# A hybrid decoder step on one core: the samples' value window put together in DRAM

## The chip, the core and the metric

The kernel runs on one core of a Trainium2 chip. Five engines work from queues of their own, each strictly in order: TensorE (PE, with its weight loads PEld), VectorE (DVE), ScalarE (ACT), GpSimd (POOL) and SyncE (SP), which here issues every DMA. The metric is the device time of one execution in microseconds (us), lower is better.

## What is computed

One inference step of two layers. Layer 0 runs sliding-window attention (8 query heads, 2 key/value heads of width 64, window 128, a learned sink per head) beside a gated delta rule; layer 1 is gated linear attention. A prompt of 2048 tokens (with 16 meta tokens in front) and 8 samples of one new token each go through both. What the change touches is the samples' attention and the cache it returns:

```python
def _swa_sample(q, k_new, v_new, k_buf, v_buf, sink):        # k_buf, v_buf: (8, 128, 2, 64)
    k = jnp.concatenate([k_buf.astype(k_new.dtype), k_new], axis=1)
    v = jnp.concatenate([v_buf.astype(v_new.dtype), v_new], axis=1)
    ...
    mask = (diff >= 0) & (diff < WINDOW)                     # the new row and the last 127 of the cache
    o = _sink_attend(q, k, v, mask, sink)
    return o.reshape(Bn, T, A_HEADS, A_HEAD_DIM), k[:, T:], v[:, T:]
```

So for each of the 8 samples a window of 128 value rows (128 floats each) is needed twice: as an operand of the attention, with a row on each partition, and as an output.

## The kernel before

The prompt is worked in four groups of 512 columns; group 0 also carries the 8 samples and 16 meta tokens, so its tiles have 536 columns, in two halves of 268. Per group: layer 0's projections (`ab_head`, `ab_rest`: key, convolution, query and gate blocks), its output projection (`ab_out`), then layer 1 (`c_main`, `c_out`). A projection (`proj`) is float32 in three passes: a weight tile is loaded raw (L270), split by ACT (L275, `wh`) and POOL (L278, `wl`, printed as L112 in the profile because a helper emits it), multiplied by PE into one of four PSUM buffers `pp`, and evacuated by DVE. In group 0 each split weight is also stored to DRAM (L245, `wd`) for the later groups. The weight pool has 8 buffers, so a raw load waits until PE is through with a tile from some blocks before.

Side work runs as generators between the blocks of a projection (`spawn`, `bulk`, with due times in `DEF_LAT`). The framework then lays out each engine's queue with a scheduler of its own, so an edit can shift instructions far from it. [...]

The samples' attention is `swa_extra`, spawned in group 0 while the fourth query and gate blocks are projected. For each half of the samples it loads the cached keys transposed (L495, `kc`, 128 partitions), then 127 cached value rows of 4 samples into partitions 0 to 126 (L498, `vc`), and then the 4 new value rows from partitions 4x to 4x+3 of `vs` into partition 127 (L499). Scores use `kc` (L527), the weighted values use `vc` (L548). Near its end it writes the outputs: cached rows 1 to 127 of each sample DRAM to DRAM (L562 for keys, L563 for values) and the new rows (L564, L570); the scheduler put L562 and L563 early, at 67.9 and 120.9 us. The new value rows `vs` come out of `ab_v` (L705), the projection of values that is evacuated at about 41 us.

Right behind L499 on SP stand the loads of the output projection: the residual X tiles (L991, 8 of 268 KB) and the raw weights of `w_abo` in two stages: 256 of 1024 columns of each of 8 blocks first, then 768 of each. In the second stage SP also stores each finished block (L1016, `x1d`).

Of the kernel before, what the change touches and what calls it, by code (L numbers as in the profile page):

```python
# [9 lines left out]
F32 = mybir.dt.float32  # L10
# [10 lines left out]
SMP = 8  # L21
# [47 lines left out]
def kernel(ctx: ExitStack, tc: tile.TileContext, ins, outs):  # L69
    nc = tc.nc  # L70
    V, A, G, T, SY = nc.vector, nc.scalar, nc.gpsimd, nc.tensor, nc.sync
# [3 lines left out]
    dr = ctx.enter_context(tc.tile_pool(name="dr", bufs=2, space=bass.MemoryType.DRAM))  # L75
# [6 lines left out]
    def nm(s):  # L82
        cnt[0] += 1
        return f"{s}_{cnt[0]}"
# [11 lines left out]
    def t512(shape=(128, 128), dt=F32):  # L96
        return wk.tile(list(shape), dt, tag="t512", bufs=4, name=nm("t5"))
# [4 lines left out]
    def cb(shape=(128, 512)):  # L102
        return pc.tile(list(shape), F32, tag="pc", name=nm("pc"))
# [4 lines left out]
    def MM(out, lhsT, rhs, start=True, stop=True):  # L108
        T.matmul(out, lhsT, rhs, start=start, stop=stop)  # L109

    def TT(out, a, b, op, eng=None):
        (eng or V).tensor_tensor(out, a, b, op=op)  # L112
# [13 lines left out]
    def bcm(ap, n):  # L126
        return ap.unsqueeze(1).to_broadcast([ap.shape[0], n] + list(ap.shape[1:]))
# [227 lines left out]
    def until(cond):  # L355
        while not cond():
            yield 0.5, 0.0
# [113 lines left out]
    def swa_extra(q, gx):  # L471
        vt = q.vt

        vm, vs = vt["m"], vt["s"]
        sc = cb()
        for h in range(8):
            MM(sc[0:16, 16 * h:16 * h + 16], QX[:, h, SMP:EX], KX[:, h // 4, SMP:EX])
        S3 = t512((128, 8, 16))[0:16]
        TT(S3, sc[0:16, 0:128].rearrange("p (h k) -> p h k", h=8), bcm(CC[0:16, C_MSK + 128:C_MSK + 144], 8), add)
        st = sm((128, 32))[0:16]  # L480
        V.tensor_reduce(st[:, 0:8], S3, axis=AX.X, op=amax)
        TT(st[:, 0:8], st[:, 0:8], RV[0:16, 0:8], amax)
        TT(S3, S3, bc(st[:, 0:8], 16), sub)
        A.activation(S3, S3, AF.Exp)
        TT(st[:, 8:16], RV[0:16, 0:8], st[:, 0:8], sub)
        A.activation(st[:, 8:16], st[:, 8:16], AF.Exp)
        V.tensor_reduce(st[:, 16:24], S3, axis=AX.X, op=add)
        TT(st[:, 16:24], st[:, 16:24], st[:, 8:16], add)
        V.reciprocal(st[:, 24:32], st[:, 16:24])
        TT(S3, S3, bc(st[:, 24:32], 16), mul)  # L490
        yield from take_in("T", 5)
        kc, vc = ([ft(shape=(128, 4, 128)) for _ in range(2)] for _ in range(2))
        for x in range(2):
            b4 = slice(4 * x, 4 * x + 4)
            SY.dma_start(kc[x][:, :, 0:127], ins["kcT"][:, b4])  # L495
            for kv in range(2):
                V.tensor_copy(kc[x][64 * kv:64 * kv + 64, :, 127], KX[:, kv, 4 * x:4 * x + 4])
            SY.dma_start(vc[x][0:127], ins["cv"][b4, 1:128, :].rearrange("b k d -> k b d"))  # L498
            SY.dma_start(vc[x][127:128, :, :], vs[4 * x:4 * x + 4, :])  # L499
        QZ = ft(shape=(128, 512))  # L500
        V.memset(QZ, 0.0)
        for kv in range(2):
            r = slice(64 * kv, 64 * kv + 64)
            dst = QZ[r, 0:504].rearrange("p (b x) -> p x b", x=72)[:, 4 * kv:4 * kv + 4, :]
            V.tensor_copy(dst, QX[:, 4 * kv:4 * kv + 4, 0:7])
            V.tensor_copy(QZ[r, 504 + 4 * kv:508 + 4 * kv], QX[:, 4 * kv:4 * kv + 4, 7])
        yield LAT["sx_1"], 0.3
        pt = cb()
        for h in range(8):
            T.transpose(pt[0:16, 16 * h:16 * h + 16], S3[:, h, :], ident[0:16, 0:16])  # L510
        PT = t512((128, 128))[0:16]
        A.copy(PT, pt[0:16, 0:128])
        yield LAT["sx_2"], 0.3
        po = cb()
        for kv in range(2):
            MM(po[64 * kv:64 * kv + 64, 0:64], vm[0:16, 64 * kv:64 * kv + 64], PT[:, 64 * kv:64 * kv + 64])
        yield from until(lambda: gx)
        for u in range(4):
            z = t512((128, 16))
            TT(z, po[:, 16 * u:16 * u + 16], GX[:, u, SMP:EX], mul)  # L520
            store_m0(q, u, z, SMP, META)

        yield 0.5, 0.1

        sc = cb()
        for b in range(8):
            MM(sc[0:64, 0:128], QZ[:, 64 * b:64 * b + 64], kc[b // 4][:, b % 4], start=(b == 0), stop=(b == 7))  # L527
        P = t512((128, 128))[0:64]
        st = sm((128, 8))[0:64]
        snk = PV[0:64, P_SNK:P_SNK + 1]  # L530
        V.tensor_copy(P, sc[0:64, 0:128])
        V.tensor_reduce(st[:, 0:1], P, axis=AX.X, op=amax)
        TT(st[:, 0:1], st[:, 0:1], snk, amax)
        TS(st[:, 1:2], st[:, 0:1], -1.0)
        A.activation(P, P, AF.Exp, bias=st[:, 1:2], accum_out=st[:, 2:3])
        A.activation(st[:, 3:4], snk, AF.Exp, bias=st[:, 1:2])
        TT(st[:, 2:3], st[:, 2:3], st[:, 3:4], add)
        V.reciprocal(st[:, 4:5], st[:, 2:3])
        TS(P, P, st[:, 4:5])
        yield LAT["sx_3"], 0.9  # L540
        pt = cb()
        T.transpose(pt[:, 0:64], P, ident[0:64, 0:64])
        PT = t512((128, 64))
        A.copy(PT, pt[:, 0:64])
        yield LAT["sx_4"], 0.1
        po = cb()
        for b in range(8):
            MM(po[:, 8 * b:8 * b + 8], vc[b // 4][:, b % 4], PT[:, 8 * b:8 * b + 8])  # L548
        pos = t512((128, 64))
        A.copy(pos, po[:, 0:64])  # L550
        pv = pos.rearrange("p (b h) -> p h b", b=8)
        for u in range(4):
            z = t512((128, 8))
            for kv in range(2):
                r = slice(64 * kv, 64 * kv + 64)
                TT(z[r], pv[r, 4 * kv + u, :], GX[r, u, 0:SMP], mul)
            store_m0(q, u, z, 0, SMP)

        give("T", 5)
        yield LAT["sx_5"], 0.9  # L560

        SY.dma_start(outs["ks"][:, 0:127, :], ins["ck"][:, 1:128, :])  # L562
        SY.dma_start(outs["vs"][:, 0:127, :], ins["cv"][:, 1:128, :])  # L563
        SY.dma_start(outs["vs"][:, 127, :], vs[0:8, :])  # L564
        kt_ = cb()
        for kv in range(2):
            T.transpose(kt_[0:8, 64 * kv:64 * kv + 64], KX[:, kv, 0:SMP], ident[0:64, 0:64])
        kn = t512((128, 128))[0:8]
        A.copy(kn, kt_[0:8, 0:128])
        SY.dma_start(outs["ks"][:, 127, :], kn)  # L570
# [110 lines left out]
    def ab_v(q):  # L681
        g, s0 = q.g, q.s0
        NS = 6 if g == 0 else 4
        BA = wk.tile([128, 6, 8], F32, tag="BA", bufs=2, name=nm("BA"))
        if g == 0:
            V.memset(BA, 0.0)
        q.vt = {}

        def ev_v(p2, slot):
            ps = t512((128, 136))  # L690
            A.copy(ps, p2[:, 136:272])
            TT(ps, ps, p2[:, 0:136], add)
            if g == 0:
                c = 4 if slot == "e" else slot
                TS(ps, ps, q.rst[:, c:c + 1])
            if slot == "e":
                e = wk.tile([128, 256], F32, tag="SM", bufs=4, name=nm("exv"))
                A.copy(e[0:EX, 0:136], ps[0:EX, 0:136])
                vm = wk.tile([128, 128], F32, tag="va", bufs=6, name=nm("vm"))
                V.memset(vm, 0.0)  # L700
                SY.dma_start(vm[0:META], e[SMP:EX, 0:128])
                SY.dma_start(BA[0:META, 0, :], e[SMP:EX, 128:136])
                V.tensor_copy(BA[0:SMP, 5, :], e[0:SMP, 128:136])
                vs = wk.tile([128, 128], F32, tag="va", bufs=6, name=nm("vs"))
                V.tensor_copy(vs[0:SMP], e[0:SMP, 0:128])  # L705
                q.vt["m"], q.vt["s"] = vm, vs
            else:
                t = wk.tile([128, 128], F32, tag="va", bufs=6, name=nm("va"))
                A.copy(t, ps[:, 0:128])
                V.tensor_copy(BA[:, slot + s0, :], ps[:, 128:136])  # L710
                q.vt[slot] = t

        ws = ([("e", 0, ev_v)] if g == 0 else []) + [(b, c0, ev_v) for b, c0 in q.wins]
        yield from proj_tok2(q, ins["w_abv"], q.H, 136, ws)
        q.vprev0 = q.vt["m"] if g == 0 else carry["v"]
        carry["v"] = q.vt[3]
        if g == NGROUPS - 1:
            SY.dma_start(outs["vp"], q.vt[3])

        q.sc = spawn(ab_scalars(q, BA, NS), "sc", 1.0)  # L720
# [1040 lines left out]
    q = new_group(0)  # L1761
    ab_first(q)
    ab_head(q)
    for g in range(groups):
# [4 lines left out]
        q = nxt  # L1769
# [109 lines left out]
```

## Time and profile before

| | us |
|---|---|
| median of 3 runs | 2281.74 |
| the runs | 2279.14 to 2282.02 |
| the profiled execution, whole | 2290.33 |
| its span in the trace | 2288.5 |
| PE busy | 2173.2 (95%) |
| DVE, ACT, POOL busy | 1204.8, 837.3, 434.7 |
| SP, from the samples' first key load (L495) to the first X load (L991) | 344.12 to 371.40 |

The profile is one execution, taken on its only core. Part 4 of its page follows the chain of work that ended last back from the end; the trace gives the same chain in order of time, each engine's instructions with the idle time ahead of them and what ended it, and busy time, granted TensorE clock and DMA share for any stretch. [...] SPq is SP's queue: the time of a row is how long SP was held by issuing that DMA.

### The profile page before, as it was taken

The page shows a single profiled execution, that of the slowest core. Times are in us where ns is not written, and L with a number is a line of the kernel's source. Part 1 is how long each engine was busy: PE and PEld are TensorE (multiplying, and loading weights), DVE is VectorE, ACT ScalarE, POOL GpSimd, SP SyncE. Part 2 cuts the span into 40 slices and gives each one's busy share as a digit, 9 for nine tenths or more (in the row PEclk, how much of TensorE's full clock was granted, in tenths as well). Part 3 has the DMA queues.
Part 4 walks back from the last instruction along what each step waited for, and adds up shares of the span by engine and source line. Part 5 has one row for each costly group of instructions (what it writes and reads, how often), then busy time and mean ns, then how long its engine had stood idle before and what let it go on. Part 6 is the DMA issues. An engine that isn't in the chain of part 4 may idle for free.

```text
span 2288.5 us, 43814 instructions
## 1 busy us (share of the span) xinstructions
PE 2173.2 (95%) x17290; PEld 1825.2 (80%) x17290; DVE 1204.8 (53%) x3361; ACT 837.3 (37%) x2235; POOL 434.7 (19%) x454
## 2 busy tenths in 40 slices
PE   7889996999999999999999999999999999999997
PEld 6777885988887977778888877778887877778886
DVE  7668765445455366654335366654335366654323
ACT  5334532444343234334233233334233234334222
POOL 3322221434342201001220000001220000001211
PEclk9989998999999999999999999999999999999998
DMA  6443333847765753264554653264554653274444
GB/s 240 158 153 132 133 110 110 286 176 241 261 242 190 259 189 112 77 218 169 179 209 152 217 189 108 77 228 160 191 196 164 212 195 103 76 242 163 170 144 156
DMA packets 162567, 399.64 MB, mean 175 GB/s; under 512 B 22010, under 2 KB 54426, under 8 KB 162346
## 3 DMA queue, kind: packets, MB, share of 16 engines
q1 hardware_dynamic: 162362, 396.84, 50.8%
q8 instruction: 136, 2.23, 0.4%
q14 instruction: 69, 0.57, 0.1%
HBM read 296.67 MB, written 101.17 MB: 174 GB/s over the span
## 4 chain that ended last, share of the span: by engine, by line
PE 73%; DVE 7%; DMA 3%; ACT 2%; issue 2%; POOL 2%; SPq 1%; DVEq 0%; POOLq 0%; ACTq 0%
PE pp L109 54%; PE pc L109 15%; DVE t L115 2%; DVE t L112 1%; DVE inv L112 1%; SPq L499 1%; POOL wl L112 1%; PE pc L931 1%; DMA raw<-in_w_cv 1%; DMA t<-in_xT 1%; PE pc L1710 1%; DMA t<-rows 1%; DVE t L119 1%; DVE t L915 0%; POOL sm L188 0%
## 5 line engine op out<-in xcount | busy, mean ns | idle before, releaser
L109 PE MATMUL pp<-t,wh 128*128 128x512 f32 (+1 forms) x4528 | 1278.7, 366 | 34.4 <-DVE t L115 15.6
L109 PEld LDWEIGHTS pp<-t,wh 128*128 128x128 f32 x4528 | 789.3, 192 | 148.7 <-DVE t L115 17.6
L109 PE MATMUL pp<-t,wl 128*128 128x512 f32 (+1 forms) x2264 | 813.7, 360 | 0.4 <-POOL wl L112 0.3
L109 PEld LDWEIGHTS pp<-t,wl 128*128 128x128 f32 x2264 | 434.3, 192 | 59.1 <-issue 1.2
L112 POOL TENSOR_TENSOR t<-t,t 128x512 fp32r<-128x512 f32 (+3 forms) x128 | 162.0, 1283 | 404.0 <-ACT t L587 265.3
L112 POOL TENSOR_TENSOR wl<-raw,wh 128x512 fp32r<-128x512 f32 (+3 forms) x138 | 173.5, 1274 | 296.6 <-PE pp L109 159.5
L115 DVE SCALAR_TENSOR_TENSOR t<-t,PV,t 128x512 f32<-128x512 f32 (+4 forms) x232 | 184.4, 802 | 64.6 <-ACT t L1012 26.4
L109 PE MATMUL pp<-wh,t 128*128 128x256 f32 (+1 forms) x1088 | 209.5, 288 | 5.1 <-DVE QKt L112 5.1
L188 POOL TENSOR_TENSOR sm<-sm,mh 128x2 f32<-128x2 f32 (+3 forms) x84 | 66.4, 790 | 673.5 <-DVE sm L115 289.7
L109 PEld LDWEIGHTS pp<-wh,t 128*128 128x128 f32 x1088 | 172.9, 191 | 7.3 <-DVE QKt L112 5.3
L115 DVE SCALAR_TENSOR_TENSOR t<-pp,t 128x512 f32<-128x512 f32 (+3 forms) x160 | 92.8, 585 | 147.2 <-PE pp L109 71.7
L109 PE MATMUL pp<-wl,t 128*128 128x256 f32 (+1 forms) x544 | 156.0, 287 | 0.0
L109 PEld LDWEIGHTS pp<-wl,t 128*128 128x128 f32 x544 | 103.8, 191 | 0.7
L275 ACT CAST wh<-raw 128x512 fp32r<-128x512 f32 (+2 forms) x122 | 67.9, 588 | 81.0 <-DMA raw<-in_w_c 23.2
L109 PE MATMUL pc<-t,t 128*128 128x128 f32 (+5 forms) x496 | 80.0, 272 | 13.4 <-DVE t L115 9.1
L109 PEld LDWEIGHTS pc<-t,t 128*128 128x128 f32 (+4 forms) x496 | 64.2, 165 | 34.6 <-issue 10.0
L112 DVE TENSOR_TENSOR t<-t,t 128x512 f32<-128x512 f32 (+4 forms) x103 | 66.7, 650 | 44.1 <-ACT t L399 43.0
L112 DVE TENSOR_TENSOR QKt<-pp,t 128x512 f32<-128x512 f32 (+1 forms) x40 | 23.2, 587 | 117.1 <-PE pp L109 110.9
L920 ACT ACTIVATE t<-t,sm 128x257 f32<-128x257 f32 x128 | 64.1, 503 | 44.0 <-DVE sm L115 43.4
L399 ACT ACTIVATE t<-t 128x512 f32<-128x512 f32 (+1 forms) x70 | 44.1, 630 | 89.8 <-DVE t L115 68.6
L854 POOL COPY hist<-t 128x3 f32<-128x3 f32 x48 | 12.0, 249 | 316.1 <-ACT t L849 282.9
L112 DVE TENSOR_TENSOR t<-pp,t 128x268 f32<-128x268 f32 (+1 forms) x90 | 44.5, 496 | 51.5 <-PE pp L109 35.6
(334 smaller groups left out, 2890.3 us busy)
## 6 DMA issues: line engine op xcount, KB each, us to landing
wh<-wd SPq DMA_DIRECT2D x157, 512.0 KB, 3.7
wl<-wd SPq DMA_DIRECT2D x157, 512.0 KB, 5.0
wd<-wh SPq DMA_DIRECT2D x55, 512.0 KB, 3.6
wd<-wl SPq DMA_DIRECT2D x55, 512.0 KB, 3.2
t<-in_xT SPq DMA_DIRECT2D x72, 256.0 KB, 4.6
raw<-in_w_ab SPq DMA_DIRECT2D x25, 512.0 KB, 3.9
raw<-in_w_c SPq DMA_DIRECT2D x16, 512.0 KB, 4.8
out_yp<-t SPq DMA_DIRECT2D x32, 256.0 KB, 2.5
```

The source lines that it names most:

```text
L109: T.matmul(out, lhsT, rhs, start=start, stop=stop)
L112: (eng or V).tensor_tensor(out, a, b, op=op)
L115: V.scalar_tensor_tensor(out, a, s, b, op0=op0, op1=op1)
L119: V.tensor_scalar(out, a, s1, None, op0=op0)
L188: G.tensor_tensor(out, x, mh[0:x.shape[0]].to_broadcast(list(x.shape)), op=ALU.pow)
L275: A.copy(hi[:, c], raw[:, c])
L399: A.activation(sq[:, :q.C], x, AF.Square)
L499: SY.dma_start(vc[x][127:128, :, :], vs[4 * x:4 * x + 4, :])
L854: G.tensor_copy(hist[:, ct], R[:, m:m + 3])
L920: A.activation(S_[:, kv], S_[:, kv], AF.Exp, bias=st[:, 2 + kv:3 + kv], accum_out=st[:, 4 + kv:5 + kv])
L931: T.transpose(pt[:, kv, x], S_[:, kv, 128 * x:128 * x + 128], ident)
L1710: T.transpose(oT[:, c], On[:, c, 128 * j:128 * j + 128], ident)
```

## The change

A DRAM tile `vwin` of 8 x 128 x 128 is filled in `ab_v`: the 127 cached rows of each sample by a copy from DRAM to DRAM, the new row from `vs`. `swa_extra` loads `vc` from it in one DMA per half over 128 partitions, and the output is one copy of the whole tile. Two DMAs of L499's form and one of L564's go, one of 508 KB DRAM to DRAM comes in.

```diff
-            SY.dma_start(vc[x][0:127], ins["cv"][b4, 1:128, :].rearrange("b k d -> k b d"))
-            SY.dma_start(vc[x][127:128, :, :], vs[4 * x:4 * x + 4, :])
+            SY.dma_start(vc[x], q.vwin[b4].rearrange("b k d -> k b d"))
...
-        SY.dma_start(outs["vs"][:, 0:127, :], ins["cv"][:, 1:128, :])
-        SY.dma_start(outs["vs"][:, 127, :], vs[0:8, :])
+        SY.dma_start(outs["vs"], q.vwin)
...
                 V.tensor_copy(vs[0:SMP], e[0:SMP, 0:128])
+
+                q.vwin = dr.tile([8, 128, 128], F32, tag="vwin", bufs=1, name=nm("vwin"))
+                SY.dma_start(q.vwin[:, 0:127, :], ins["cv"][:, 1:128, :])
+                SY.dma_start(q.vwin[:, 127, :], vs[0:SMP])
```

From the middle of layer 0 of group 0 on, the queues of PE are the same but for a handful of rows; what moves lies in group 0's first 120 us and in its output projection. Three places follow. Numbers behind names are the program's own and differ between the two programs; line numbers of the changed program are 1 lower from L500 to L563, 2 lower from L565 to L705, and 2 higher from L706 on (L706 and L707 are its two copies into `vwin`).

SP, at the samples' keys and values in group 0, before (`t_4640`, `t_4641` are the two `kc`, `t_4642`, `t_4643` the two `vc`, `t_4705` the first X tile of the output projection):

```order
L245 DMA wd_4853<-wh_4849 128x256
L495 DMA t_4640<-in_kcT 128x4x127
L498 DMA t_4642<-in_cv 127x4x128
L499 DMA t_4642<-vs_427 1x4x128
L495 DMA t_4641<-in_kcT 128x4x127
L498 DMA t_4643<-in_cv 127x4x128
L499 DMA t_4643<-vs_427 1x4x128
L991 DMA t_4705<-in_xT 128x536
L270 DMA raw_4881<-in_w_abo 128x256
L245 DMA wd_4853<-wl_4850 128x256
L991 DMA t_4706<-in_xT 128x536
L270 DMA raw_4957<-in_w_abo 128x256
```

and now:

```order
L245 DMA wd_4854<-wh_4850 128x256
L495 DMA t_4643<-in_kcT 128x4x127
L498 DMA t_4645<-vwin_429 128x4x128
L495 DMA t_4644<-in_kcT 128x4x127
L498 DMA t_4646<-vwin_429 128x4x128
L993 DMA t_4706<-in_xT 128x536
L270 DMA raw_4882<-in_w_abo 128x256
L245 DMA wd_4854<-wl_4851 128x256
L993 DMA t_4707<-in_xT 128x536
L270 DMA raw_4958<-in_w_abo 128x256
L993 DMA t_4708<-in_xT 128x536
```

The two one-partition copies are gone from between the key loads and the X and weight loads; the rest stands in the same order.

SP, in the second stage of the output projection, before (`raw_5348` to `raw_5525` are raw weights of blocks 3 to 6, `x1d` the stores of blocks 0 to 3):

```order
L270 DMA raw_5348<-in_w_abo 128x768
L245 DMA wd_4853<-wh_5293 128x768
L1016 DMA x1d_4703<-t_5172 128x536
L245 DMA wd_4853<-wl_5294 128x768
L270 DMA raw_5407<-in_w_abo 128x768
L1016 DMA x1d_4703<-t_5229 128x536
L245 DMA wd_4889<-wh_5352 128x768
L245 DMA wd_4889<-wl_5353 128x768
L270 DMA raw_5466<-in_w_abo 128x768
L1016 DMA x1d_4703<-t_5288 128x536
L245 DMA wd_4965<-wh_5411 128x768
L245 DMA wd_4965<-wl_5412 128x768
```

and now:

```order
L1018 DMA x1d_4704<-t_5172 128x536
L270 DMA raw_5348<-in_w_abo 128x768
L245 DMA wd_4854<-wh_5293 128x768
L1018 DMA x1d_4704<-t_5229 128x536
L245 DMA wd_4854<-wl_5294 128x768
L270 DMA raw_5407<-in_w_abo 128x768
L245 DMA wd_4890<-wh_5352 128x768
L245 DMA wd_4890<-wl_5353 128x768
L1018 DMA x1d_4704<-t_5288 128x536
L270 DMA raw_5466<-in_w_abo 128x768
L245 DMA wd_4966<-wh_5411 128x768
L245 DMA wd_4966<-wl_5412 128x768
```

Each raw load, which stood ahead of a block's store, now stands behind it, and so behind DVE's evacuation of that block.

ACT, in the first 35 us (`t_222` is the row of norms that the first evacuations need, `wh_532` or `wh_535` a weight, `wv` the value weights, `KX`, `kh` copies of the key projection), before:

```order
L155 ACTIVATE t_146<-t_81 128x536
L455 CAST wv_390<-raw_392 128x4x136
L455 CAST wv_391<-raw_392 128x4x136
L387 COPY t_222<-pc_223 128x512
L391 COPY t_222<-pc_229 128x24
L275 CAST wh_532<-raw_526 128x512
L790 COPY KX_207<-t_268 64x24 x2
L784 CAST kh_56_194<-t_268 64x16
L784 CAST kh_58_196<-t_268 64x16
L784 CAST kh_56_194<-t_268 64x512
L784 CAST kh_58_196<-t_268 64x512
L275 CAST wh_532<-raw_526 128x512
```

and now:

```order
L155 ACTIVATE t_146<-t_81 128x536
L387 COPY t_222<-pc_223 128x512
L391 COPY t_222<-pc_229 128x24
L792 COPY KX_207<-t_268 64x24 x2
L786 CAST kh_56_194<-t_268 64x16
L786 CAST kh_58_196<-t_268 64x16
L786 CAST kh_56_194<-t_268 64x512
L786 CAST kh_58_196<-t_268 64x512
L846 COPY XS_210<-t_351 128x8
L455 CAST wv_390<-raw_392 128x4x136
L455 CAST wv_391<-raw_392 128x4x136
```

The casts of the value weights moved from ahead of the norm row to behind the copies of the key projection; their second halves on POOL moved with them. On SP the new copy of 508 KB (L706) stands at place 14, behind the first raw weight loads and ahead of the load of the value weights; the copy of the new rows (L707) stands behind the two small copies out of `exv` that were there before.

## Rows read from the trace of the kernel before

**Rows 1.** The page, part 4: the chain that ended last, by line.
```profile
PE pp L109 54%; PE pc L109 15%; DVE t L115 2%; DVE t L112 1%; DVE inv L112 1%; SPq L499 1%; POOL wl L112 1%; PE pc L931 1%; DMA raw<-in_w_cv 1%; DMA t<-in_xT 1%; PE pc L1710 1%; DMA t<-rows 1%; DVE t L119 1%; DVE t L915 0%; POOL sm L188 0%
```
**Rows 2.** The chain in order of time, 330 to 390 us: start, us, what.
```profile
345.05 12.19 SPq L499
...
358.17 13.19 SPq L499
...
371.40 4.34 DMA t<-in_xT
...
381.72 0.30 PE pc L542
```
**Rows 3.** Stretches: us, busy by engine (count), granted clock, DMA share, GB/s.
```profile
362.00:371.00 9.00, 2.47 (x16) 2.07 (x14) 0.00 (x0) 0.00 (x0) 0.00 (x0) 0.69 0.08 20
...
376.00:382.00 6.00, 5.75 (x26) 5.39 (x26) 4.09 (x18) 1.86 (x6) 1.72 (x2) 0.50 0.62 197
...
414.00:436.00 22.00, 22.00 (x182) 22.00 (x181) 10.94 (x20) 11.16 (x21) 8.75 (x9) 1.00 0.94 328
```
**Rows 4.** Timeline, 354 to 377 us: start, us, instruction [idle before, what ended it].
```profile
354.25 0.66 PE L109 MATMUL pc<-t,va 128*64 128x128 f32 x8
...
361.65 1.76 PE L109 MATMUL pc<-t,t 128*64 128x128 f32 x7 [4.07 <-DMA t<-in_kcT]
...
375.76 0.44 DVE L115 SCALAR_TENSOR_TENSOR t<-pp,t 128x268 f32<-128x268 f32 x1 [17.55 <-DMA t<-in_xT]
...
376.25 0.82 PE L109 MATMUL pp<-t,wh 128*128 128x268 f32 x2 [11.78 <-DVE t L115]
```
**Rows 5.** The page, part 6: DMA issues, count, KB each, us to landing.
```profile
raw<-in_w_abo SPq DMA_DIRECT2D x8, 384.0 KB, 3.5
...
t<-in_sdn SPq DMA_DIRECT2D x8, 256.0 KB, 7.0
...
raw<-in_w_abo SPq DMA_DIRECT2D x8, 128.0 KB, 2.4
```
**Rows 6.** Timeline of SP, 67 to 122 us.
```profile
69.09 1.01 SPq L1570 DMA_DIRECT2D t<-in_sdn  x2
...
120.88 1.09 SPq L563 DMA_DIRECT2D out_vs<-in_cv  x1
```
**Rows 7.** Timeline of SP, ACT, POOL and DVE, 386 to 423 us: the output projection's loads and stores.
```profile
386.02 0.42 SPq L270 DMA_DIRECT2D raw<-in_w_abo  x1
...
389.88 0.38 SPq L270 DMA_DIRECT2D raw<-in_w_abo  x1
...
391.12 0.39 ACT L275 CAST wh<-raw 128x256 fp32r<-128x256 f32 x1
...
411.14 1.05 SPq L270 DMA_DIRECT2D raw<-in_w_abo  x1
413.77 0.32 SPq L1016 DMA_DIRECT2D x1d<-t  x1
...
415.25 0.93 ACT L275 CAST wh<-raw 128x384 fp32r<-128x384 f32 x2 [0.18 <-DMA raw<-in_w_abo]
...
415.90 1.99 POOL L112 TENSOR_TENSOR wl<-raw,wh 128x384 fp32r<-128x384 f32 x2 [1.97 <-ACT wh L275]
...
422.16 0.44 DVE L115 SCALAR_TENSOR_TENSOR t<-pp,t 128x268 f32<-128x268 f32 x1 [1.43 <-PE pp L109]
```
**Rows 8.** Timeline, 19 to 55 us: POOL, DVE and PE in the start.
```profile
19.43 2.68 POOL L112 TENSOR_TENSOR wv<-raw,wv 128x544 fp32r<-128x544 f32 x2 [0.50 <-ACT wv L455]
...
19.58 1.23 DVE L221 CAST SEL<-CC 4x4 fp32r<-4x4 f32 x1
...
20.84 1.83 DVE L112 TENSOR_TENSOR t<-t,t 128x536 f32<-128x536 f32 x1
...
23.42 0.39 PE L109 MATMUL pp<-t,wh 128*128 128x268 f32 x1 [1.87 <-DVE t L115]
...
53.98 0.40 PE L109 MATMUL pc<-graw,CC 128*128 128x20 f32 x2 [3.92 <-DVE graw L119]
```

## The prediction

> **What bounds the kernel now.** I read the page's chain by line first [rows 1]. Nearly 70% of the span hangs on PE's matrix products, so a gain has to come from a place where PE stands still. One entry is not an engine's work at all: SP's queue held by L499, 1% of 2288.5 us, some 25 us. The chain in order of time shows where [rows 2]: two issues of L499, 12.19 and 13.19 us, 25.4 in all, with nothing between them but the second half's key and value issues, then the 4.34 us of the first X tile of the output projection. So the end of the chain waits there for a queue, not for bytes.
>
> Next, who waits [rows 4]. PE stands 4.07 us until the second half's keys are in (they were issued behind the first L499) and 11.78 us for DVE's evacuation, which itself stands 17.55 us for the X tile (issued behind the second L499). PE's idle time there is 4.07 + 11.78 = 15.85 us. Third, the clock [rows 3]. [...] Before, with PE busy, 8 products of 128x128 took 0.66 us; the 7 behind the 4.07 us wait took 1.76 [rows 4]. The stall is paid twice, as idle time and as slow products behind it.
>
> Why SP is held: in 362 to 371 us the DMA engines were 8% busy with 20 GB/s [rows 3], little more than one of sixteen. 254 KB of cached rows at 20 GB/s are 12.7 us, near the 12.19 and 13.19 us of the two holds [rows 2]. So I read the hold as L499 waiting, at its issue, for room behind a load (L498) that one DMA engine carries alone. The trace does not show which of the two lines is at fault; that does not matter for this change, which removes both forms.
>
> **The change part by part.**
>
> *The two holds go.* In the new order key, value, key, value and X loads stand in a row on SP. The X tile, issued at 371.40 before, would be issued near 346 (five issues of about 0.45 us from 344.1) and land 4.34 us later [rows 2], near 350.4. DVE's idle time of 17.55 us ended at 375.76, so it has nothing before 358.2 to wait with; X is there 8 us earlier, and the second keys, issued beside it and counted at the same 4.34, 7 us before PE asks for them at 357.6 (361.65 less 4.07). Both PE waits lose their cause: **15.9 us**.
>
> *The clock stays up.* Behind the first wait 16 products run from 361.65 to 364.46 (376.25 less 11.78), 2.81 us, against 2 x 0.66 = 1.32 at the full clock: 1.5. Behind the second PE works 376.25 to 381.72 [rows 2, 4], 5.47 us at 0.50; half of it, 2.7, is the clock's. Together **4.2 us**.
>
> *What is late next.* L542, the samples' last product ahead of the next stretch, stands behind DVE's mask and ACT's exponential of the scores. With slow products these run beside PE; with fast ones part of them shows. Bounds 0 and 2.7 (all that the clock gives there); walking the order with the durations of before I get L542 near 363, which costs **1.5 us** of the 20.1.
>
> *First stage of the output projection.* The raw weights issued at 386.02 and 389.88 now stand behind the store of the sample keys and further X loads, about 4 us later for each. The second of these has cover: 386.02 + 2.4 us [rows 5] = 388.4 is the landing of the first, ACT splits it at 391.12 [rows 7], so 2.7 us are spare; 4 less 2.7 is 1.3 for each of two blocks, **2.6 us** given back. Bounds: 0 (PE has other products there) and 8.
>
> *Second stage.* Each raw load, 384 KB, now follows a block's store and so DVE's evacuation. Take the store at 413.77 [rows 7]; the load can be issued 0.9 us later, when a weight store stands between. The weights are wanted as the second block after it is evacuated, 422.16 less 0.1, some 8.3 us after the store. Needed: 0.9, the landing, half of ACT's 0.93 and half of POOL's 1.99 [rows 7]: 2.4 plus the landing. That is 5.9 with the 3.5 of that load [rows 5], 6.5 with the 4.1 seen at 411.14 to 415.25 [rows 7]. It fits with 1.8 us to spare: **0**. The cover is thin, since the DMA engines are 94% busy there [rows 3]; the rivals hold the price.
>
> *The start.* The value weights are split later on ACT and POOL. Two additions of POOL, 19.43 to 22.11, lie beside two DVE steps of unusual length (1.23 us for a 4x4 cast, 1.83 for a sum), and PE waits 1.87 us behind them [rows 8]. Moved away, I count that wait as gone: **1.9 us** gained. The value projection at some 33 us can in turn wait for those weights, and the wait of 3.92 us at 53.98 (on numbers that come out of that projection) can shrink or grow; neither is shown in the trace, so the start as a whole has bounds of 4 either way, nearest to the one row that names its cause.
>
> *The DRAM copies.* L706 moves 508 KB. A copy of that form held SP 1.09 us [rows 6]; at SP's place 14 there is slack of many us until the value projection's small copies at about 41 us, so it is hidden. The two halves of L498 read what was written 300 us before. L707 is one small issue at 41 us, ahead of one raw load, 0.3 to 0.6 us, hidden unless that load is late already. The output copy replaces one equal in size, and L564 goes: 0.
>
> The row of 362 to 371 us shows about one engine's share for 127 partitions [rows 3]. [...]
>
> **Sum.** 15.9 + 4.2 - 1.5 - 2.6 + 1.9 = 17.9 us. The profiled execution took 2290.3, 8.6 us over the median of 2281.7; the stall is a fixed queue time in every execution, so I carry the difference over: 2281.7 - 17.9 = 2263.8, **2264 us**.
>
> **The rivals.**
>
> *Given back in the second stage.* If the raw loads behind the stores land in 7.0 us, as other loads do in busy places [rows 5], 9.4 us are needed against 8.3: 1.1 us for each of 8 blocks, 8.8. The gain is 9: **2273**. For it: 94% DMA share [rows 3]. Against: the 3.5 and 4.1 us measured on these very loads.
>
> *Slower.* The same place, with a higher price: each us over a landing of 5.9 us costs 8 us, so the gain is used up at 5.9 + 17.9/8 = 8.1 us. At 9 us 3.1 x 8 = 24.8 go: about **2289**. No row of these loads is near 8.1.
>
> *More.* The start also gains the 3.92 us wait [rows 8] and the first stage gives nothing back: 17.9 + 3.9 + 2.6 = 24.4, **2257**. For it: the value projection's evacuation moves ahead of the work that feeds that wait; against: its weights come later.
>
> *The hold stays.* If SP is held whenever a load scatters 4 samples over partitions, the new L498 holds it too, and the time stays at **2281**. Against: two loads of similar size and full width, `in_sdn`, were issued in 1.01 us together [rows 6].
>
> **How the numbers follow.** Forecast 2264 (by itself 2258 to 2270): 0.60. Given back, 2273: 0.17. More, 2257: 0.13. Hold stays, 2281: 0.07. Slower, 2289: 0.03. The range goes from 2255, below the "more" case, to 2274, past the "given back" case; the last two cases are left out, and about half of what is uncertain in the start. A measurement of this kernel can tell about 0.2%, 4.6 us, from no change. Faster by more than that: 0.60 + 0.17 + 0.13 = 0.90; within it 0.07; slower 0.03.
>
> **What would show it.** L499's rows gone from the chain, the two L498 issues below 1 us each; PE with no idle time of several us between the scores and L542, with the clock at 1.00 there; L542 near 363 plus whatever the start shifts; no PE wait over 1 us in the second stage of the output projection; the 1.87 us wait near 23 us gone. The prediction is wrong if SP still stands over 5 us at L498, if PE waits there for another cause (scores, X), or if the second stage shows PE waits on `wl` block after block.

## The result: about 1% faster, the larger part from SP's queue and the rest from a start that was not meant to change

| | before, median us | this, median us | ratio, 95% interval |
|---|---|---|---|
| the changed kernel | 2282.02 | 2265.83 | 0.9909 (0.9888 to 0.9930) |
| again, another job | 2286.56 | 2262.35 | 0.9893 (0.9875 to 0.9912) |
| a third time | 2284.62 | 2259.62 | 0.9893 (0.9868 to 0.9917) |

The forecast was 2264 with a range of 2255 to 2274, and a gain of 17.9 us. The first comparison gave 2265.83; its medians lie 16.2 us apart, inside the interval of its ratio. The ratios say 20.8 us (0.0091 x 2282), 24.5 and 24.4, so the sign and the place were right, and the sum was some 5 us too small if the three are taken together.

**The profile after.** In the chain that ended last, L499 is gone from the list by line [rows 1], and by engine SP's queue has no share left:

```profile
PE 68%; DVE 6%; DMA 3%; ACT 2%; issue 2%; POOL 1%; SPq 0%; DVEq 0%; POOLq 0%; ACTq 0%
```

SP's timeline at the samples' loads, to hold against the 12.19 and 13.19 us of [rows 2]:

```profile
333.09 0.43 SPq L495 DMA_DIRECT2D t<-in_kcT  x1
333.57 0.55 SPq L498 DMA_DIRECT2D t<-vwin  x1
334.17 0.51 SPq L495 DMA_DIRECT2D t<-in_kcT  x1
334.71 0.51 SPq L498 DMA_DIRECT2D t<-vwin  x1
335.26 0.50 SPq L993 DMA_DIRECT2D t<-in_xT  x1
```

Five issues of about half a microsecond, and the X tile goes out 2.2 us after the first key load; before, it was 27.3 us (344.12 to 371.40). PE in the same place, to hold against [rows 4]:

```profile
345.37 1.85 PE L109 MATMUL pc<-t,t 128*64 128x128 f32 x15
...
347.69 0.52 PE L109 MATMUL pp<-t,wh 128*128 128x268 f32 x2
...
349.38 0.52 PE L109 MATMUL pp<-t,wh 128*128 128x268 f32 x2 [0.20 <-DVE sm L119]
...
351.51 0.24 PE L541 MATMUL pc<-CC,t 64*128 64x64 f32 x1 [0.25 <-DVE t L119]
```

The 15 products run on without the 4.07 us wait in their middle, the projection follows without the 11.78 us wait, and L541 (L542 of before) is waited for 0.25 us. Two stretches (columns as in [rows 3]): the first is the place of the holds, to set against the granted clocks of 0.69 and 0.50 there (shares of the full clock); the second is the second stage of the output projection, to set against the last row there:

```profile
343.00:352.00 9.00, 8.54 (x84) 7.28 (x84) 8.49 (x45) 4.27 (x14) 1.94 (x2) 1.00 0.51 162
...
381.00:410.00 29.00, 28.43 (x228) 28.00 (x227) 15.96 (x25) 13.58 (x25) 15.08 (x12) 1.00 0.83 281
```

**Where the time went, by stage.** Five rows that exist in every version cut the trace: PE's products behind its wait of some 8 us (162.49 before, 153.49 after), PE's product behind its wait of 1.17 us (328.81, 317.70), L542, the first store of an output block (410.18, 381.32) and the seventh (435.90, 409.24). The last two columns are `loads_only` and `fill_only`, two experiments below that each carry one half of the change.

| stretch, us | before | after | loads only | fill only |
|---|---|---|---|---|
| start, to the products behind the 8 us wait | 162.5 | 153.5 | 163.3 | 152.6 |
| on to the product behind the 1.17 us wait | 166.3 | 164.2 | 165.4 | 169.3 |
| on to L542 (holds, scores) | 52.8 | 33.8 | 33.8 | 52.7 |
| on to the first store (first stage) | 28.5 | 29.8 | 29.8 | 28.4 |
| on to the seventh store (second stage) | 25.7 | 27.9 | 26.5 | 25.8 |
| on to the end | 1852.6 | 1847.1 | 1844.0 | 1846.4 |

The third row is the change that was meant: 19.0 us. The first row is 9.0 us that were not meant. The second and the last row hold the same products in all four, in the same order but for a handful; what differs there is the clock (granted in the second row: 0.93 before, 0.96 after; PE busy in the last: 1804.2 and 1800.3 us), and small waits that change from execution to execution (in the last row PE's idle times add up to 40.9 us before and 34.9 in `fill_only`). So the two profiled executions, 2288.5 and 2256.4 us of span, lie 32.1 us apart, which is more than the change is worth.

**The start.** Here is the wait that is gone. Before, on PE:

```profile
116.84 0.77 PE L109 MATMUL pc<-t,t 128*128 128x128 f32 x2 [7.21 <-DVE t L115]
```

and the DVE rows that lead up to it, first the samples' recurrent step (L1596), then the convolution taps that PE waits for:

```profile
98.93 0.55 DVE L1596 COPY t<-pc 8x384 f32<-8x384 f32 x1 [5.27 <-PE pc L1594]
...
109.06 1.61 DVE L115 SCALAR_TENSOR_TENSOR t<-t,PV,t 128x528 f32<-128x528 f32 x1 [1.35 <-ACT t L851]
```

After, the same three places:

```profile
109.06 0.38 PE L109 MATMUL pc<-t,t 128*128 128x128 f32 x2
```

```profile
90.33 0.55 DVE L1598 COPY t<-pc 8x384 f32<-8x384 f32 x1
...
100.86 0.77 DVE L115 SCALAR_TENSOR_TENSOR t<-t,PV,t 128x528 f32<-128x528 f32 x1 [1.69 <-ACT t L853]
```

PE reaches the product at about the same moment as before (109.6 with the wait taken off 116.84, now 109.06), but DVE begins its taps 8.2 us earlier, because the samples' step ahead of them in its queue came 8.6 us earlier. PE's order says why. The waiting product is the 893rd on PE in both traces, behind 464 block products (those into `pp`). The samples' products that feed DVE's step (L1594, L1596 after) stand behind 422 block products before and behind 360 now. Before, the 64x64 products of another piece of side work follow them with no block product between; after, 24 block products stand between the two:

```profile
98.40 0.49 PE L1594 MATMUL pc<-CC,sm 128*8 128x128 f32 x3
...
101.00 0.68 PE L109 MATMUL pc<-t,t 64*64 64x64 f32 x8
```

```profile
88.39 0.49 PE L1596 MATMUL pc<-CC,sm 128*8 128x128 f32 x3
...
94.98 0.68 PE L109 MATMUL pc<-t,t 64*64 64x64 f32 x8
```

The 62 block products by which the samples' moved up take about 0.123 us each (three in the 0.37 us from 108.32 to 108.69 in the trace after), 7.6 us together. Where the wait stood the granted clock was lower too: two stretches of 16 us around the place, before at 0.68 and after at 1.00:

```profile
108.00:124.00 16.00, 8.79 (x48) 8.05 (x47) 12.84 (x28) 6.18 (x16) 5.38 (x5) 0.68 0.81 284
```

```profile
100.00:116.00 16.00, 15.00 (x116) 14.21 (x116) 12.70 (x29) 7.00 (x17) 6.08 (x5) 1.00 0.76 256
```

Against that stands a new wait. The value weights are split on POOL from 30.74 on, and PE, which before met them ready, waits:

```profile
32.59 1.26 PE L109 MATMUL pp<-wv,t 128*128 128x272 f32 x8 [3.03 <-POOL wv L112]
```

The wait of 1.87 us at 23.42 [rows 8] is gone, and that of 3.92 at 53.98 is 0.99 (at 52.46).

### The profile page after: what moved, and what is told of

It reads as the page before. It is cut to its first block, busy times and chain, and to the rows that moved or that the text cites. A ratio compares the mean times of both kernels' runs of the same rounds, so it can differ in the third digit from the quotient of the medians.

```text
span 2256.4 us, 43806 instructions
## 1 busy us (share of the span) xinstructions
PE 2158.9 (96%) x17290; PEld 1810.5 (80%) x17290; DVE 1202.6 (53%) x3361; ACT 836.6 (37%) x2235; POOL 441.9 (20%) x454
## 4 chain that ended last, share of the span: by engine, by line
PE 68%; DVE 6%; DMA 3%; ACT 2%; issue 2%; POOL 1%; SPq 0%; DVEq 0%; POOLq 0%; ACTq 0%
PE pp L109 51%; PE pc L109 14%; DVE t L115 1%; DVE t L112 1%; DVE inv L112 1%; PE pc L933 1%; DMA t<-x1d 1%; DMA t<-in_xT 1%; DMA raw<-in_w_cv 1%; PE pc L1712 1%; POOL wl L112 0%; DVE t L119 0%; DMA t<-rows 0%; POOL sm L188 0%; DVE t L1100 0%
## 5 line engine op out<-in xcount | busy, mean ns | idle before, releaser
L112 POOL TENSOR_TENSOR t<-t,t 128x512 fp32r<-128x512 f32 (+3 forms) x128 | 162.6, 1286 | 398.4 <-ACT t L585 258.8
L112 POOL TENSOR_TENSOR wl<-raw,wh 128x512 fp32r<-128x512 f32 (+3 forms) x138 | 180.0, 1321 | 277.3 <-PE pp L109 152.6
L115 DVE SCALAR_TENSOR_TENSOR t<-t,PV,t 128x512 f32<-128x512 f32 (+4 forms) x232 | 181.2, 788 | 66.6 <-ACT t L853 27.3
L109 PEld LDWEIGHTS pc<-t,t 128*128 128x128 f32 (+4 forms) x496 | 63.0, 162 | 24.2 <-DVE t L115 5.1
```

The costliest lines, as they stand in the source:

```text
L115: V.scalar_tensor_tensor(out, a, s, b, op0=op0, op1=op1)
```

## The experiments

**Which half of the change brings what.** Three programs that each take one half, in one job, with the changed kernel beside them. `loads_only`:

```diff
-            SY.dma_start(vc[x][0:127], ins["cv"][b4, 1:128, :].rearrange("b k d -> k b d"))
-            SY.dma_start(vc[x][127:128, :, :], vs[4 * x:4 * x + 4, :])
+            SY.dma_start(vc[x], ins["cv"][b4, 0:128, :].rearrange("b k d -> k b d"))
```

> The kernel before, but each value load takes 128 partitions straight from the cache in one DMA (rows 0 to 127 of it, so the window is off by one and the new row is left out of the samples' attention), and the copy of four rows into one partition is gone. No copy into vwin, so the first 120 us keep the order of before; the output projection has the order of the changed kernel. Theory 'the holds' (the two holds of SP are what the change is worth): 16 to 20 us faster than before, ratio 0.991 to 0.993; in its trace no PE wait over 2 us between 340 and 370 us, the clock at 1.00 there, and the wait of some 7 us near 117 us still present. Rival 'the start' (most comes from the re-ordered first 120 us, where the two traces differ by 11 us): 5 to 8 us faster, ratio 0.9965 to 0.998.

Measured: ratio 0.9938 (0.9919 to 0.9957), 14.2 us faster, between the two forecasts; the interval, 9.8 to 18.5 us, reaches into that of 'the holds' and not into that of 'the start'. In its trace PE waits nowhere from 330 to 390 us for as much as 0.9 us, and the start's wait is there:

```profile
117.83 0.55 PE L109 MATMUL pc<-t,t 128*128 128x128 f32 x1 [7.21 <-DVE t L115]
```

`fill_only`, the changed kernel with the loads of before:

```diff
-            SY.dma_start(vc[x], q.vwin[b4].rearrange("b k d -> k b d"))
+            SY.dma_start(vc[x][0:127], ins["cv"][b4, 1:128, :].rearrange("b k d -> k b d"))
+            SY.dma_start(vc[x][127:128, :, :], vs[4 * x:4 * x + 4, :])
```

> The changed kernel with its copies into vwin and its output from vwin, but with the value loads of before (127 partitions, then four rows into one). The first 120 us have the order of the changed kernel, the output projection that of before. Theory 'the holds': both holds of 12 to 13 us are back in the trace and PE's waits of 4 and 12 us with them; the time is within 5 us of before (ratio 0.998 to 1.002). Rival 'the start': 8 to 11 us faster (ratio 0.995 to 0.9965), the 7 us wait near 117 us gone in its trace and the holds still there.

Measured: 0.9954 (0.9940 to 0.9967), 10.5 us faster. Both holds are back, and with them both of PE's waits:

```profile
338.10 11.98 SPq L499 DMA_DIRECT2D t<-vs  x1
...
351.01 13.18 SPq L499 DMA_DIRECT2D t<-vs  x1
```

```profile
354.52 1.75 PE L109 MATMUL pc<-t,t 128*64 128x128 f32 x7 [3.94 <-DMA t<-in_kcT]
...
369.16 0.59 PE L109 MATMUL pp<-t,wh 128*128 128x268 f32 x1 [11.82 <-DVE t L115]
```

The time is the one that 'the start' gave for this run, so neither theory, as put, holds for both: neither half carries the gain alone. They add up: 14.2 + 10.5 = 24.7, against 24.5 for the whole change in the same job.

`fill_late` writes the two copies at the head of the samples' attention and not behind the value projection:

```diff
+        q.vwin = dr.tile([8, 128, 128], F32, tag="vwin", bufs=1, name=nm("vwin"))
+        SY.dma_start(q.vwin[:, 0:127, :], ins["cv"][:, 1:128, :])
+        SY.dma_start(q.vwin[:, 127, :], vs[0:SMP])
...
-                q.vwin = dr.tile([8, 128, 128], F32, tag="vwin", bufs=1, name=nm("vwin"))
-                SY.dma_start(q.vwin[:, 0:127, :], ins["cv"][:, 1:128, :])
-                SY.dma_start(q.vwin[:, 127, :], vs[0:SMP])
```

> The changed kernel with the two copies into vwin written at the head of the samples' attention instead of behind the value projection. They stand later on SP (places 43 and 67), and PE's order in the first 120 us is that of before; the loads, the output and the output projection are those of the changed kernel. Theory 'the holds': 16 to 20 us faster than before, level with the changed kernel within 5 us, the 7 us wait near 117 us present. Rival 'the start': 5 to 8 us faster than before, 8 to 11 us slower than the changed kernel.

Measured: 0.9912 (0.9888 to 0.9936), 20.1 us faster; the wait near 117 us is there (7.15 us). Its interval overlaps both that of `loads_only` and that of the changed kernel, so the time alone decides nothing; the stages show which half it has: 33.8, 29.8 and 26.5 us from the third row of the table on, as in `loads_only`.

`changed_again` is the changed kernel, for a second trace:

> The changed kernel once more, for a second trace and a tighter ratio on the same chip as its variants. Both theories: 14 to 18 us faster than before (ratio 0.992 to 0.994). The two traces so far differ by 32 us, twice the difference of the medians; if that is chance in the clock, this trace shows more lowered clock than the first (some 10 us of the 24 us by which the clock's losses of the two traces differ), with the same waits; if it is in the waits, this trace shows a wait of several us that the first does not have.

Measured: 24.5 us faster, more than expected. The waits are those of the first trace (3.03 at the value weights, and at 112.12 only the 0.90 that the first trace has as 0.89). On the clock the expectation missed: adding up 10 x (1 - granted clock) over all stretches of 10 us gives 36.5 us against 33.2 in the first trace, 3.3 more and not 10, for a span 2.9 us longer. The third trace of the changed kernel has 46.9 and a span of 2268.4, 12.0 longer than the first. So what separates these three traces is mostly the clock.

**What holds SP.** Three variants of the kernel before. `split` loads the 127 rows as 112 and 15 and keeps the four-row copy:

```diff
-            SY.dma_start(vc[x][0:127], ins["cv"][b4, 1:128, :].rearrange("b k d -> k b d"))
+            SY.dma_start(vc[x][0:112], ins["cv"][b4, 1:113, :].rearrange("b k d -> k b d"))
+            SY.dma_start(vc[x][112:127], ins["cv"][b4, 113:128, :].rearrange("b k d -> k b d"))
```

> The kernel before, with the 127 cached rows loaded in two DMAs, 112 and 15 partitions, and the copy of four rows into one partition kept as it was. No vwin. Theory 'room behind one engine' (the four-row copy is held at its issue because 127 partitions were loaded by one DMA engine): the four-row copy is issued in under 1.5 us, both PE waits of 4 and 12 us are gone, and the time is that of the run with full-width loads, 14 us faster than before (ratio 0.992 to 0.996), with the 7 us wait near 117 us still there. Rival 'the four-row copy itself' (SBUF to SBUF, four partitions into one): the holds of 12 to 13 us stay and the time is within 3 us of before.

The four-row copies (now L500) are issued in 0.68 and 0.63 us:

```profile
349.75 0.55 SPq L498 DMA_DIRECT2D t<-in_cv  x1
350.35 0.50 SPq L499 DMA_DIRECT2D t<-in_cv  x1
350.89 0.68 SPq L500 DMA_DIRECT2D t<-vs  x1
```

So a copy of four rows into one partition is not slow in itself. The time is 0.9953 (0.9938 to 0.9967), 10.7 us faster; the interval overlaps that of `loads_only`, so the time alone does not tell the two apart. In the trace the stretch to L542 falls to 34.2 us, but the one to the first store grows to 33.9, since the order there is another one and PE waits in it:

```profile
378.51 0.67 PE L932 MATMUL pc<-CC,t 128*128 128x128 f32 x4 [2.84 <-DVE t L119]
```

`row_from_dram` fills partition 127 from DRAM:

```diff
-            SY.dma_start(vc[x][127:128, :, :], vs[4 * x:4 * x + 4, :])
+            SY.dma_start(vc[x][127:128, :, :], ins["cv"][b4, 0:1, :].rearrange("b k d -> k b d"))
```

> The kernel before with one edit: partition 127 of each value tile is filled with four rows of the cache in DRAM (row 0 of each sample) and not from vs, so the new row is left out of the samples' attention. Every engine's order is that of before. Theory 'room behind one engine': the source does not matter, this one-partition DMA is held 12 to 13 us as well, and the time is within 5 us of before. Rival 'the four-row copy itself': it is issued in about 0.5 us and PE's waits go.

```profile
343.89 11.91 SPq L499 DMA_DIRECT2D t<-in_cv  x1
...
356.73 13.26 SPq L499 DMA_DIRECT2D t<-in_cv  x1
```

The source makes no difference to the hold. The one execution took 2278.01, 6.3 us below the median of before in that job (2284.26), so the expected 5 us was missed. `swapped` puts the four-row copy ahead of the 127-row load:

```diff
-            SY.dma_start(vc[x][0:127], ins["cv"][b4, 1:128, :].rearrange("b k d -> k b d"))
             SY.dma_start(vc[x][127:128, :, :], vs[4 * x:4 * x + 4, :])
+            SY.dma_start(vc[x][0:127], ins["cv"][b4, 1:128, :].rearrange("b k d -> k b d"))
```

> The kernel before with the four-row copy written ahead of the 127-partition load of the same tile; nothing else moves. Theory 'room behind one engine': the first four-row copy is issued in about 0.5 us; the DMA behind the 127-partition load, the second half's key load, is held some 12 us in its place, and the next one behind the second load (the X tile) as well: two holds of 12 to 13 us, each one place further on, and the time is within 5 us of before. Rival 'the four-row copy itself': the holds stay with the four-row copies.

```profile
337.05 0.67 SPq L498 DMA_DIRECT2D t<-vs  x1
337.77 0.41 SPq L499 DMA_DIRECT2D t<-in_cv  x1
338.23 11.51 SPq L495 DMA_DIRECT2D t<-in_kcT  x1
349.78 0.81 SPq L498 DMA_DIRECT2D t<-vs  x1
350.64 0.42 SPq L499 DMA_DIRECT2D t<-in_cv  x1
351.11 12.74 SPq L991 DMA_DIRECT2D t<-in_xT  x1
```

The hold moved to whatever stands behind the 127-partition load: the key load, then the X tile, both full-width loads that are issued in half a microsecond elsewhere. During the first of these holds the DMA engines moved 22 GB/s at a share of 0.08:

```profile
339.00:349.00 10.00, 9.57 (x86) 8.74 (x87) 9.23 (x37) 4.64 (x15) 1.98 (x2) 1.00 0.08 22
```

So the cause is L498, and L499 was only the next in line. Nor does the hold come from further ahead in the queue: the third issue from the first key load on, held 12.19 us before, goes out in 0.41 us here, and the queue ahead of that key load is the same. The one execution took 2279.15, 5.1 us below the median of before, just outside the expected 5. The share of 0.08 is that of 16 DMA engines, by which an estimated 1.3 of them were busy (0.08 x 16); and `split`, which loads the same rows as 112 and 15, has no hold (0.68 and 0.63 us). From these two I read that one engine carries the load over 127 partitions; why that load holds SP and those over 128, 112 and 15 do not, no run shows. That the issue of the next DMA has to wait for room behind the load is my reading of these rows; no row shows the room itself.

**Which of the two copies moves the start.** `big_early` leaves only the 508 KB copy behind the value projection, `small_early` only the eight-row copy; the other one is written at the head of the samples' attention:

```diff
+        SY.dma_start(q.vwin[:, 127, :], vs[0:SMP])
...
                 SY.dma_start(q.vwin[:, 0:127, :], ins["cv"][:, 1:128, :])
-                SY.dma_start(q.vwin[:, 127, :], vs[0:SMP])
```

> The changed kernel with only the 508 KB copy left behind the value projection; the copy of the eight new rows is written at the head of the samples' attention. The value weights are split late as in the changed kernel. If the order that the 508 KB copy brings is what removes the 7 us wait near 117 us, the trace lacks that wait and the time is level with the changed kernel (22 to 25 us faster than before, ratio 0.989 to 0.9905). If it comes from the eight-row copy, the wait is there and the time is that of the version with both copies late, or worse by the 3 us wait for the value weights (14 to 20 us faster, ratio 0.991 to 0.994).

Measured: 0.9894 (0.9872 to 0.9916), 24.2 us faster; the product near 111 us is not waited for, and the 3.01 us wait for the value weights is there. Its interval overlaps that of `fill_late`, so what the new order of the start is worth does not come out of these two times.

> The changed kernel with only the copy of the eight new rows left behind the value projection and the 508 KB copy written at the head of the samples' attention (place 44 on SP). Expected if the 508 KB copy's place brings the new order: the wait of 7 us near 117 us is back, no 3 us wait for the value weights, and the start ends (PE behind its 8 us wait near 155 to 163 us) at 160 to 163 us as in the kernel before. Rival: if the eight-row copy brings it, the wait near 117 us is missing and the start ends at 152 to 156 us.

Its trace has the wait back and no wait for the value weights:

```profile
112.23 0.55 PE L109 MATMUL pc<-t,t 128*128 128x128 f32 x1 [8.09 <-DVE t L115]
```

So the 508 KB copy brings the new order. The expected end of the start, 160 to 163 us, was missed: 155.6, with 5.67 us of wait there and another 2.22 at 161.09. Part of the difference is another wait that shrank, that at 53.98 before (3.92 us), to 0.82; what moved it I did not isolate. More of it is the clock: against `fill_late`, where the start ends at 160.1, PE is idle 0.9 us less ahead of that end, and the losses over the first 150 us, by the sum above, are 8.5 us against 11.9. One execution took 2265.57.

**A version with both good orders.** `two_copies` cuts the 508 KB copy in two:

```diff
-                SY.dma_start(q.vwin[:, 0:127, :], ins["cv"][:, 1:128, :])
+                SY.dma_start(q.vwin[:, 0:112, :].rearrange("b k d -> k b d"), ins["cv"][:, 1:113, :].rearrange("b k d -> k b d"))
+                SY.dma_start(q.vwin[:, 112:127, :].rearrange("b k d -> k b d"), ins["cv"][:, 113:128, :].rearrange("b k d -> k b d"))
```

> The changed kernel with the copy into vwin cut in two, 112 and 15 rows of each sample, row by row over the samples, at the same place in the code. In the order this leaves the split of the value weights early, as in the kernel before, and keeps the samples' first recurrent products ahead of the fourth block's, as in the changed kernel. Expected if both order effects are as read: no wait of 3 us for the value weights near 32 us and no wait of 7 us near 117 us, 0 to 4 us faster than the changed kernel on the same chip (ratio to before 0.987 to 0.9905). Rival: the small copies collide with the first weight loads, PE waits several us more in the first 30 us, and it is level with the changed kernel or 2 to 5 us slower.

> The changed kernel on the same chip as its version with two copies: 20 to 25 us faster than before (ratio 0.989 to 0.9915), its trace with the 3 us wait for the value weights near 32 us and without the wait near 117 us.

Measured: 0.9887 (0.9862 to 0.9911) against 0.9893 (0.9868 to 0.9917) for the changed kernel in the same job: no difference that can be measured. In its trace neither of the two waits exists, and its start is the shortest of all, 150.6 us; but the small wait ahead of the first weights is back:

```profile
23.79 0.39 PE L109 MATMUL pp<-t,wh 128*128 128x268 f32 x1 [1.88 <-DVE t L115]
```

`before_again` is the kernel before, for a second trace:

> The kernel before, for a second trace. Both holds of SP (12 and 13 us), both PE waits (4 and 12 us) and the 7 us wait near 117 us are there again. The first trace took 8.6 us more than the median; if that is chance in the granted clock, the waits are the same within 0.5 us and the clock's losses are smaller by about that amount.

Holds and waits are the same (4.33, 11.79 and 7.22 us); the clock's losses by the sum above are 62.0 against 57.8, not smaller, and this execution too took longer than the median (2288.64 against 2284.62). So the 8.6 us by which the first profiled execution of before lay over its median stay unexplained by this pair. `row_from_dram` and `swapped`, whose PE queues are that of before row for row, had spans of 2276.2 and 2277.3 us with losses of 50.1 and 44.5, so the clock is the likeliest reason, though not a shown one.

## Why the prediction held, term by term

- **The holds and PE's 15.9 us of waits: right.** Both waits are gone in every trace without the 127-partition load, and present in every trace with it. The reading that one DMA engine carries that load fits the share of 0.08 and `split`, and the line at fault, which the prediction left open, is L498.
- **The clock, 4.2, and what is late next, -1.5: right together.** The stretch to L542 fell by 19.0 us against 18.6 in the sum (15.9 + 4.2 - 1.5). The rows separate it. PE's waits gave 15.9. The 24 products around the first wait take 2.32 us (345.37 to 347.69) against 1.09 + 2.81 before, 1.6 less, as in the sum (1.5). Behind the second wait PE reaches L541 in 3.82 us (347.69 to 351.51), against 5.40 before (376.25 to 381.65), 1.6 less; the sum had 2.7 less 1.5. Of what is late next only 0.25 us shows as a wait at L541. Its start, 351.51, is 362.6 when the 11.1 us by which the stretch begins earlier are added; the forecast was near 363.
- **First stage, -2.6: right in sign, half the size, and not by the way that was priced.** The stretch to the first store is 1.3 us longer in the changed kernel and in `loads_only` alike. The two raw loads did go out later (7.7 and 11.8 us behind L541, against 4.4 and 8.2 behind L542 before), but PE's only wait for a weight there is 0.20 us; its longer waits are for other things, 1.32 us for DVE (at 359.35) and 1.28 for POOL:

```profile
373.61 0.39 PE L109 MATMUL pp<-t,wl 128*128 128x268 f32 x1 [0.20 <-POOL wl L112]
...
379.95 0.39 PE L109 MATMUL pp<-t,wh 128*128 128x268 f32 x1 [1.28 <-POOL t L112]
```

  The stretch also holds more products, 217 (215 in `loads_only`) against 209. So the raw loads had cover enough, and what the stage gave back has other causes.
- **Second stage, 0: nearly.** The stretch of six blocks is 0.8 us longer in `loads_only`, `changed_again` and `changed_third` (26.5 against 25.7), and 2.2 in the first trace of the changed kernel. The rivals "given back" (8.8) and "slower" (24.8) fell: 1.8 us of cover was enough.
- **The start, +1.9: the mis-sized term.** It measured 7.7 us: the start ends at 155.0 on average in five traces with the changed kernel's place for the 508 KB copy (`after` 153.5, `changed_again` 155.1, `changed_third` 157.7, `fill_only` 152.6, `big_early` 156.1) and at 162.7 in six without it (`before` 162.5, `before_again` 163.7, `loads_only` 163.3, `split` 163.8, `row_from_dram` 162.6, `swapped` 160.0; `fill_late` and `small_early` are left out, as the 8 us wait that ends the stretch is in two pieces there). The named wait of 1.87 us did go, and the doubt about the value weights came true at 3.03 us. The step that failed is that the sum priced the start by the value weights and by the waits at 23.42 and 53.98 alone, and put nothing on PE's wait of 7.21 us near 117 us. That wait's product stands in the same place of PE's queue in both programs, but its feeder, the samples' step on DVE, had moved by 62 products. The bound of 4 us either way was too narrow for the same reason. Nor is the gain that wait alone. Ahead of the 8 us wait, with 1146 products in every trace, PE's idle times add up to 25.2 us on average in the six and to 22.2 in the five: only 3.0 us less, since waits of 3.03 and of about 1 us came in. The clock's losses over the first 150 us, by the sum above, are 13.1 and 5.4. So most of the 7.7 us is the same products at a higher clock, which the prediction counted for the holds and not for the start.
- **The copies, 0: right.** L706 held SP 0.78 us at 8.43 in the trace of after, and the output from `vwin` 0.53. The new copy does not show in the first waits: PE is through its first wait of 1.3 us at 19.98 us, against 19.55 before. What did cost 3 us in the start was the later split of the value weights.
- **The sum.** 19.0 - 1.3 - 0.8 = 16.9 for the loads (timed alone: 14.2, interval 9.8 to 18.5), and 7.7 for the start (timed alone: 10.5, interval 7.5 to 13.7), together 24.6; the forecast had 16.0 and 1.9. The likeliest case's range of 2258 to 2270 held all three medians. That the first of them came within 2 us of the forecast is luck in part: the ratio of the same runs gives 2.9 us more than the sum, and the two later ones 6.5.
- **Rivals.** "The hold stays" fell with the first trace. "More" (24.4 us) is the size that came, but by another way: the first stage did give something back, and the start gained by the wait near 117 and by the clock, not only by the wait at 53.98.

## What to carry to other kernels

When a queue is held by a small DMA, look at the one ahead of it: here two loads over 127 partitions held SP for 25 us in all, and whichever DMA stood behind them, small or large, was held (11.51 to 13.26 us). Count the clock with every wait that goes or stays (here 0.50 behind the 11.78 us wait, and 1.00 in the same place without it), also where the edit was not aimed. Price an edit that moves a scheduler's order by the feeders of each wait, not by the place of the waiting instruction, and look above all at the waits near the edit that have nothing to do with it. And size a gain of 1% by timed rounds of half-changes, as one pair of profiles here lay 32.1 us apart, more than the change is worth.

## What the runs showed of the hardware that was not expected

- A full-width load that is issued in 0.43 us elsewhere held its queue for 11.51 us behind a load over 127 partitions, while the 16 DMA engines together were busy for a share of 0.08 (`swapped`, 339 to 349 us).
- The same program's clock losses vary from execution to execution: three traces of the changed kernel lost 33.2, 36.5 and 46.9 us by the sum above with the same waits, and their spans follow (2256.4, 2259.3, 2268.4).
